# A planner of the instruction order that counts DMA issue time and orders in several passes

## The chip, the cores and the metric

The kernel runs on one core of one Trainium2 chip. The time is the device time of one execution in microseconds (us), median of several runs. TensorE (PE in the profile), VectorE (DVE), ScalarE (ACT), GpSimd (POOL) and SyncE (SP, which issues all the DMAs here) run side by side, each through its own list of instructions in a fixed order. So when an instruction waits, everything behind it on the same engine waits too.

## What is computed

One encoder layer on 1024 + 256 = 1280 tokens of width 1024, in float32: a SwiGLU half step, a token mixing step, a second SwiGLU half step, and a final norm.

```python
h = x + 0.5 * _swiglu(_rmsnorm(x, ffn1_norm), ffn1_w_gate, ffn1_w_up, ffn1_w_down)
...
# mixing: banded attention with a sink (8 heads) beside bidirectional
# retention (4 heads) through one input and one output projection
...
def _swiglu(x, w_gate, w_up, w_down):
    return (jax.nn.silu(x @ w_gate) * (x @ w_up)) @ w_down
```

The hidden width of each SwiGLU is 2816, that is 22 tiles of 128.

## The kernel before

**Arithmetic.** The tokens stand in chunks of 512, 512 and 256 columns (called chunk 0, 1 and 2). Each large product is made of three fast matmuls: both operands are split into a high and a low part (`split`: a cast on ACT makes `xh` or `whi`, a subtraction on DVE makes `xl` or `wlo`), and PE adds xh·whi, xl·whi and xh·wlo. In the two FFNs, seven products stand for eight (`combos` makes sums of activations, `seven` sums of weights), so DVE and ACT have work on every weight tile: `raw` (loaded), `s1` to `s4` (sums, made on DVE), `whi`, `wlo`.

**FFN.** For each of 11 pairs of hidden tiles, gate and up are computed (a wave writes the PSUM banks `pa`; ACT and DVE evict them to `o11`, `o21`, `o22` and `s`), then the activation is split and stored to DRAM in pieces named `a1_<pair>_<piece><h or l>` for FFN1 and `a2_...` for FFN2 (pieces 1, 2, 3, 8, 9, 10 and so on; the profile calls them `a_1l`). Later the down product loads pieces back as `xa` tiles, multiplies them into banks `pb`, and DVE adds those into the residual `h`. The pieces of the last pair are `a1_10_...` and `a2_10_...`; they are stored at the place where gate and up end and the down product starts, called transition 1 (FFN1) and transition 2 (FFN2) below.

**Mixing.** `project` makes the input projection (`lin` products into `pa`), `attention` makes scores, probabilities `prob`, their transposes (PE, into `pb`) and their copies `pt`, `retention` works on blocks, `out_unit` is the output projection.

**Order.** None of this is emitted as it is written. `Weaver` records each operation as an `Op` (`record`, line 172) with a modelled cost (`cost`, line 141) and latency. `order` (line 219) then simulates the five engines: it takes again and again the operation that can start first, and on one engine, among those that could start within `SLACK` of the engine's free time, the one that stands earliest in the program (the heap `now`). It also simulates the slots of the two SBUF pools (77 of 128x512, 66 of 128x256) and of the eight PSUM banks: an operation that needs a new tile waits until a slot is free, and a slot is freed when the last reader of its old tile is done. A DMA reads its `raw` or writes its `a_` piece, so the slot of a stored `xh` or `xl` is free only when its store has landed. SP may run at most `AHEAD` = 300 operations ahead of PE. `emit` (line 364) emits each engine's instructions in the order found. Every instruction of the profile therefore has line 372.

Of the kernel before, what the change touches and what calls it, by code (L numbers as in the profile page):

```python
# [89 lines left out]


class Op:
    __slots__ = ("eng", "calls", "cost", "lat", "bufs", "deps", "idx", "wait", "succ", "ready", "allocs", "kind", "at")

    def __init__(self, eng):
        self.eng, self.calls, self.cost, self.lat, self.bufs, self.deps = eng, [], 0.0, 0.13, {}, set()
# [3 lines left out]
class Weaver:  # L100
# [3 lines left out]

    MARGIN = 0.4
    AHEAD = 300
    ENG = {"tensor": "PE", "vector": "DVE", "scalar": "ACT", "gpsimd": "POOL", "sync": "SP"}

    def __init__(self, tc):
# [30 lines left out]
    @staticmethod  # L140
    def cost(eng, method, a, k, outs, ins):
        n = outs[0].box[3] - outs[0].box[2] if outs else 0
        if eng == "tensor":
            if method == "transpose":
                return 0.107
            r = ins[0].buf.args[2] == F32R
            if r:
                return n / 2400 + 0.0136

            side = outs[0].box[1] - outs[0].box[0] <= 64  # L150
            return max((2.2 if side else 4) * n / 2400, 0.11 if n == 1 else 0.213)
        m = max([n] + [v.box[3] - v.box[2] for v in ins])
        ps = any(v.buf.psum for v in ins)
        if eng == "scalar":
            if a[2:3] == (AF.Identity,):
                return 0.3
            return (0.05 if ps else 0.09) + m * 0.00084 + (0.19 if "accum_out" in k else 0)
        if eng == "gpsimd":
            return 0.3 + n * 0.17
        if method in ("tensor_copy", "tensor_scalar") and not ps:  # L160
            return 0.07 + n * 0.00052 + 0.06 * (len(ins) > 1)
        if method == "tensor_scalar":
            return 0.06 + n * 0.00104 + 0.06 * (len(ins) - 1)
        if method == "tensor_tensor_reduce":
            return 0.13 + n * 0.00104
        if method == "scalar_tensor_tensor":
            return 0.12 + n * 0.00107
        if method == "reciprocal":
            return 0.07 + n * 0.0064
        return 0.07 + m * 0.00104  # L170

    def record(self, calls):
        op = Op(self.ENG[calls[0][0]])
        op.idx = len(self.ops)
        op.calls = calls
        for eng, method, a, k in calls:
            vals = [v for v in list(a) + list(k.values()) if isinstance(v, View)]
            outs = [k["out"]] if "out" in k else [a[0]]
            if k.get("accum_out") is not None:
                outs.append(k["accum_out"])  # L180
            outs = [v for v in outs if isinstance(v, View)]
            ins = [v for v in vals if not any(v is x for x in outs)]
            if method == "dma_start":
                v = (outs + ins)[0]
                nb = (v.box[1] - v.box[0]) * (v.box[3] - v.box[2]) * 4
                op.cost, op.lat, op.kind = 0.05, 2.2, nb
            else:
                op.cost += self.cost(eng, method, a, k, outs, ins)
                f = a[2] if method == "activation" and len(a) > 2 else None
                if f in (AF.Silu, AF.Exp):  # L190
                    op.kind = f
            for views, wr in ((ins, False), (outs, True)):
                for v in views:
                    b = v.buf
                    box = (0, P, 0, b.width) if b.psum else v.box
                    keep = []
                    for x in b.accesses:
                        (p0, p1, c0, c1), i, w = x

                        w = w or b.psum and self.ops[min(i, op.idx - 1)].eng != op.eng  # L200
                        hit = p0 < box[1] and box[0] < p1 and c0 < box[3] and box[2] < c1
                        if hit and (wr or w) and i != op.idx:
                            op.deps.add(i)
                        inside = box[0] <= p0 and p1 <= box[1] and box[2] <= c0 and c1 <= box[3]
                        if not (wr and inside) or i == op.idx:
                            keep.append(x)
                    keep.append((box, op.idx, wr))
                    b.accesses = keep
                    if id(b) not in op.bufs:
                        op.bufs[id(b)] = b  # L210
                        b.left += 1
                        if b.order is None and b.tag is not None:
                            t = self.tags.setdefault(b.tag, {"cap": b.bufs, "bufs": [], "free": [0.0] * b.bufs})
                            b.order = len(t["bufs"])
                            t["bufs"].append(b)
                            op.allocs.append(b)
        self.ops.append(op)

    def order(self):
        import heapq  # L220

        ops = self.ops

        for t in self.tags.values():
            t["seq"], t["live"], t["next"], t["done"] = [0] * len(t["bufs"]), set(), 0, [False] * len(t["bufs"])
# [39 lines left out]
        first = [0]  # L265
# [11 lines left out]
        free = dict.fromkeys(engs, 0.0)  # L277

        later = {e: [] for e in engs}
        now = {e: [] for e in engs}  # L280
# [7 lines left out]
        while len(out) < len(ops):  # L288
            best = None
            for e in engs:  # L290
                lim = free[e] + SLACK
                while later[e] and later[e][0][0] <= lim:
                    heapq.heappush(now[e], heapq.heappop(later[e])[1])
                held = []
                pick = None
                while now[e]:
                    i = heapq.heappop(now[e])
                    if may(ops[i]):
                        pick = (max(free[e], ops[i].ready), i)
                        heapq.heappush(now[e], i)  # L300
                        break
                    held.append(i)
                    if len(held) > 40:
                        break
                for i in held:
                    heapq.heappush(now[e], i)
                if pick is None:
                    for r, i in sorted(later[e])[:40]:
                        if may(ops[i]):
                            pick = (r, i)  # L310
                            break
                if pick is not None:
                    op = ops[pick[1]]
                    start = pick[0]
                    for b in op.allocs:
                        start = max(start, min(self.tags[b.tag]["free"]))
                    if best is None or start < best[0]:
                        best = (start, pick[1], e)
            start, i, e = best
            op = ops[i]  # L320
            if i in now[e]:
                now[e].remove(i)
                heapq.heapify(now[e])
            else:
                later[e].remove((op.ready, i))
                heapq.heapify(later[e])
            for b in op.allocs:
                t = self.tags[b.tag]
                f = min(t["free"])
                t["free"].remove(f)  # L330
                start = max(start, f)
                t["live"].add(b.order)
                t["done"][b.order] = True
                while t["next"] < len(t["done"]) and t["done"][t["next"]]:
                    t["next"] += 1
            cost = op.cost
            if e == "ACT" and op.kind is not None and op.kind != table:
                cost += 1.3
                table = op.kind
            end = start + cost  # L340
            op.at = start
            free[e] = end
            if e == "SP":
                dma = max(dma, end) + op.kind / 390e3
                end = dma
            end += op.lat
            for b in op.bufs.values():
                b.left -= 1
                b.end = max(b.end, end)
                if b.left == 0 and b.tag is not None:  # L350
                    self.tags[b.tag]["free"].append(b.end)
                    self.tags[b.tag]["live"].discard(b.order)
            for s in op.succ:
                x = ops[s]
                x.wait -= 1
                late = 0.0 if x.eng != "PE" else -op.lat if e == "PE" else self.MARGIN
                x.ready = max(x.ready, end + late)
                if x.wait == 0:
                    heapq.heappush(later[x.eng], (x.ready, s))
            out.append(op)  # L360
# [875 lines left out]
```

## Time and profile before

| | |
|---|---|
| runs | 2379.52, 2381.1, 2383.1 us, median 2381.1 |
| profiled execution | 2384.64 us, its span 2382.7 us |
| granted TensorE clock, mean | 0.981 |
| busy | PE 2300.1 us, DVE 1664.0, ACT 1011.8, POOL 28.2 |

The span is the time from the first to the last instruction of the core; the profiled execution's own time is 1.9 us more, and 3.5 us above the median of the runs. Idle time of PE is where a change of order can give or take, as long as PE's work itself stays.

### The profile page before, as it was taken

What the parts mean: (1) busy time and instruction counts of PE and PEld (TensorE: products, weight loads), DVE (VectorE), ACT (ScalarE), POOL (GpSimd) and SP (SyncE); (2) the same over time, 40 slices, a digit from 0 to 9 for tenths busy, and PEclk for the clock granted to TensorE, in tenths of its full rate; (3) what the DMA queues carried; (4) which work ended last, traced back from release to release, by engine and by line L of the source; (5) the groups of instructions that cost most, each with busy time, mean ns of one, the idle gap of its engine ahead of it and who ended that gap; (6) DMA issues with size and microseconds to landing.
All of it is one profiled execution on the core that took longest, in us unless ns stands there. A gap on an engine that the chain in (4) does not pass through costs nothing.

```text
span 2382.7 us, 35970 instructions
## 1 busy us (share of the span) xinstructions
PE 2300.1 (97%) x12354; PEld 1948.1 (82%) x12354; DVE 1664.0 (70%) x3639; ACT 1011.8 (42%) x2297; POOL 28.2 (1%) x31
## 2 busy tenths in 40 slices
PE   7999999999799999999999999999999999989998
PEld 6888888888688888886777878888888888868887
DVE  8677766675777866655677767956776766677866
ACT  6444444443222235235667555534444444322311
POOL 0000000000000000000000000000000000000000
PEclk8999999999899999999999999999999999999999
DMA  4233343338865443230115254223443335876622
GB/s 161 95 123 123 132 147 116 111 114 290 281 197 191 142 154 107 70 106 32 32 43 180 85 168 144 66 100 126 140 153 111 114 122 188 278 250 202 191 81 89
DMA packets 230296, 330.77 MB, mean 139 GB/s; under 512 B 25824, under 2 KB 113760, under 8 KB 230112
## 3 DMA queue, kind: packets, MB, share of 16 engines
q1 hardware_dynamic: 230112, 328.47, 41.2%
q8 instruction: 97, 1.59, 0.3%
q14 instruction: 87, 0.71, 0.1%
HBM read 226.65 MB, written 101.71 MB: 138 GB/s over the span
## 4 chain that ended last, share of the span: by engine, by line
PE 88%; DVE 3%; DMA 3%; ACT 3%; issue 1%; SPq 1%; POOL 0%; POOLq 0%; DVEq 0%; ACTq 0%
PE pa L372 61%; PE pb L372 26%; ACT prob L372 2%; DMA raw<-wf 1%; SPq L372 1%; DVE prob L372 1%; DVE xn L372 1%; DVE wlo L372 1%; ACT whi L372 0%; DVE o L372 0%; DMA xa<-a_7l 0%; PE pc L372 0%; DVE xl L372 0%; ACT pt L372 0%; DVE h L372 0%
## 5 line engine op out<-in xcount | busy, mean ns | idle before, releaser
L372 PE MATMUL pa<-xh,whi 128*128 128x512 f32 (+1 forms) x2576 | 921.6, 358 | 10.3 <-ACT whi L372 3.8
L372 PE MATMUL pa<-xh,wlo 128*128 128x512 f32 (+1 forms) x2576 | 911.8, 354 | 6.1 <-DVE wlo L372 6.0
L372 PE MATMUL pa<-xl,whi 128*128 128x512 f32 (+1 forms) x2576 | 912.1, 354 | 5.6 <-DVE xl L372 5.6
L372 PEld LDWEIGHTS pa<-xh,whi 128*128 128x128 f32 x2576 | 491.5, 191 | 86.7 <-ACT whi L372 8.6
L372 PEld LDWEIGHTS pa<-xh,wlo 128*128 128x128 f32 x2576 | 490.2, 190 | 78.9 <-DVE wlo L372 12.4
L372 PEld LDWEIGHTS pa<-xl,whi 128*128 128x128 f32 x2576 | 491.3, 191 | 69.4 <-DVE xl L372 6.5
L372 PE MATMUL pb<-xa,whi 128*128 128x512 f32 (+1 forms) x1968 | 526.3, 356 | 21.3 <-DVE h L372 18.6
L372 ACT CAST whi<-raw 128x256 fp32r<-128x256 f32 (+1 forms) x676 | 304.3, 473 | 444.1 <-PE pa L372 216.0
L372 PEld LDWEIGHTS pb<-xa,whi 128*128 128x128 f32 x1968 | 349.8, 191 | 77.2 <-DVE h L372 21.9
L372 DVE TENSOR_TENSOR wlo<-raw,whi 128x256 fp32r<-128x256 f32 (+1 forms) x676 | 327.6, 505 | 107.7 <-PE pa L372 53.3
L372 ACT CAST whi<-s 128x256 fp32r<-128x256 f32 x464 | 184.2, 406 | 412.6 <-DVE s L372 211.9
L372 PE MATMUL pb<-xa,wlo 128*128 128x512 f32 (+1 forms) x984 | 348.7, 354 | 3.2 <-DVE wlo L372 3.2
L372 DVE SCALAR_TENSOR_TENSOR h<-pb,h 128x512 f32<-128x512 f32 (+1 forms) x408 | 245.9, 623 | 61.8 <-PE pb L372 59.4
L372 DVE TENSOR_TENSOR wlo<-s,whi 128x256 fp32r<-128x256 f32 x464 | 191.5, 423 | 104.6 <-PE pa L372 53.2
L372 PEld LDWEIGHTS pb<-xa,wlo 128*128 128x128 f32 x984 | 187.5, 191 | 30.9 <-DVE wlo L372 4.4
L372 DVE TENSOR_TENSOR s<-raw,raw 128x256 f32<-128x256 f32 x232 | 97.9, 422 | 86.2 <-PE pa L372 78.7
L372 DVE TENSOR_TENSOR s<-s,raw 128x256 f32<-128x256 f32 x232 | 97.1, 423 | 52.0 <-PE pa L372 34.7
L372 DVE TENSOR_TENSOR o<-o,pa 128x512 f32<-128x512 f32 x120 | 82.2, 685 | 68.9 <-PE pa L372 36.4
L372 ACT ACTIVATE sq<-h 128x512 f32<-128x512 f32 (+1 forms) x96 | 50.4, 555 | 117.1 <-DVE h L372 101.1
L372 ACT CAST xh<-s 128x512 fp32r<-128x512 f32 (+1 forms) x114 | 60.3, 537 | 81.2 <-DVE s L372 56.9
L372 DVE TENSOR_TENSOR xl<-s,xh 128x512 fp32r<-128x512 f32 (+1 forms) x114 | 65.1, 585 | 19.5 <-ACT xh L372 12.7
L372 DVE TENSOR_TENSOR sq<-sq,sq 128x512 f32<-128x512 f32 (+1 forms) x93 | 55.7, 600 | 17.1 <-ACT sq L372 12.8
(126 smaller groups left out, 1644.0 us busy)
## 6 DMA issues: line engine op xcount, KB each, us to landing
raw<-wf SPq DMA_DIRECT2D x464, 128.0 KB, 2.5
raw<-w_in SPq DMA_DIRECT2D x132, 256.0 KB, 3.1
raw<-w_out SPq DMA_DIRECT2D x48, 256.0 KB, 3.1
raw<-wf SPq DMA_DIRECT2D x32, 256.0 KB, 3.6
h<-xT SPq DMA_DIRECT2D x32, 256.0 KB, 5.4
a_1h<-xh SPq DMA_DIRECT2D x22, 256.0 KB, 2.0
a_2h<-xh SPq DMA_DIRECT2D x22, 256.0 KB, 2.1
a_1l<-xl SPq DMA_DIRECT2D x22, 256.0 KB, 2.3
```

Of the source, the lines that this page charges most:

```text
L372: i = getattr(getattr(self.nc, eng), method)(*[r(x) for x in a], **{m: r(x) for m, x in k.items()})
```

## The change

The instructions stay the same ones, 11830 on PE, 3541 on DVE, 2209 on ACT, 27 on POOL and 1598 on SP as the two orders list them; only their order differs. The planner's costs change: an issued DMA keeps SP for 0.47 us where it was 0.05, and lands 2.0 us after its bytes where it was 2.2; a matmul counts as narrow by the smaller of its output's and its operand's partitions; an ACT operation with a tile as scale costs 0.1 more; `bn_stats` costs 0.3. And the order is found in up to four passes. After a pass, `due` walks back from the planned start of each PE operation and gives every other operation the time by which it has to start. The next pass ranks such an operation by the furthest PE operation of the program that was started by then, if that is earlier than its own place. The pass with the shortest modelled span is taken.

```diff
@@ -147,20 +148,23 @@
-            side = outs[0].box[1] - outs[0].box[0] <= 64
+            side = min(outs[0].box[1] - outs[0].box[0], ins[0].box[1] - ins[0].box[0]) <= 64
...
-            return (0.05 if ps else 0.09) + m * 0.00084 + (0.19 if "accum_out" in k else 0)
+            return (0.05 if ps else 0.09) + m * 0.00084 + (0.19 if "accum_out" in k else 0) + (
+                0.1 if isinstance(k.get("scale"), View) else 0)
...
+        if method == "bn_stats":
+            return 0.3
...
-                op.cost, op.lat, op.kind = 0.05, 2.2, nb
+                op.cost, op.lat, op.kind = 0.47, 2.0, nb
...
     def order(self):
+        best, prio = None, list(range(len(self.ops)))
+        for _ in range(self.PASSES):
+            out = self.arrange(prio)
+            if best is None or self.span < best[0]:
+                best = self.span, out
+            due = self.due()
+            at = sorted((op.at, op.idx) for op in self.ops if op.eng == "PE")
+            times, k = [], 0
+            front = 0
+            for t, i in at:
+                front = max(front, i)
+                times.append((t, front))
...
+            prio = []
+            for op in self.ops:
+                if op.eng == "PE" or due[op.idx] is None:
+                    prio.append(op.idx)
+                else:
+                    j = bisect.bisect(times, (due[op.idx], 1 << 60)) - 1
+                    prio.append(min(op.idx, times[max(j, 0)][1]))
+        self.span, out = best
+        return out
+
+    def due(self):
+        due = [None] * len(self.ops)
+        for op in reversed(self.ops):
+            t = None
+            for i in op.succ:
+                s = self.ops[i]
+                x = s.at if s.eng == "PE" else due[i]
+                if x is not None and (t is None or x < t):
+                    t = x
+            if t is not None:
+                due[op.idx] = t - op.cost - op.lat
+        return due
+
+    def arrange(self, prio):
...
-                    heapq.heappush(now[e], heapq.heappop(later[e])[1])
+                    i = heapq.heappop(later[e])[1]
+                    heapq.heappush(now[e], (prio[i], i))
```

Three places show what the new order does. In the rows, the last number of a name is only a counter of the compiled program; the first one names the tile and is the same in both orders.

The first is SP's list at transition 1, where the stores of the last pair stand between the loads of the down product's first pieces. Before:

```order
L372 DMA a1_10_1l_6773<-xl_1605_6760 128x512
L372 DMA xa_1745_6775<-a1_2_5l_2235 128x512
L372 DMA xa_1746_6777<-a1_1_4h_1624 128x512
L372 DMA xa_1747_6779<-a1_1_4l_1653 128x512
L372 DMA xa_1748_6788<-a1_2_4h_2222 128x512
L372 DMA xa_1749_6790<-a1_2_4l_2240 128x512
L372 DMA xa_1754_6792<-a1_1_8h_1436 128x256
L372 DMA xa_1755_6794<-a1_1_8l_1449 128x256
L372 DMA xa_1756_6796<-a1_2_8h_2007 128x256
L372 DMA a1_10_8l_6800<-xl_1613_6786 128x256
L372 DMA xa_1757_6802<-a1_2_8l_2029 128x256
```

With the change, from the first of those stores on:

```order
L433 DMA xa_1754_6716<-a1_1_8h_1425 128x256
L433 DMA xa_1755_6722<-a1_1_8l_1451 128x256
L433 DMA raw_1762_6727<-wf1 128x256
L433 DMA raw_1763_6735<-wf1 128x256
L433 DMA a1_10_1h_6744<-xh_1604_6729 128x512
L433 DMA a1_10_1l_6746<-xl_1605_6739 128x512
L433 DMA a1_10_8h_6755<-xh_1612_6753 128x256
L433 DMA xa_1728_6760<-a1_2_1h_2018 128x512
L433 DMA xa_1729_6770<-a1_2_1l_2034 128x512
L433 DMA a1_10_8l_6779<-xl_1613_6766 128x256
L433 DMA xa_1732_6791<-a1_2_2h_2124 128x512
L433 DMA xa_1733_6799<-a1_2_2l_2139 128x512
```

The store of `xl_1605` moved from SP's row 440 to 428, that of `xl_1613` from 449 to 432; the loads of pieces `a1_2_1` and `a1_2_2` and all that follow now stand behind them. Transition 2 shows the same: the store of `xh_5543` moved from row 1374 to 1344 and that of `xl_5544` from 1383 to 1346.

The second is DVE's list at the start of FFN2, where `wlo_4127` is the low part of the first gate weight, and the `xl_41..` before it are the low parts of the combined activations. Before:

```order
L372 TENSOR_TENSOR xl_4112_16837<-n2_4108_16823,xh_4111_16831 128x512
L372 TENSOR_TENSOR xl_4114_16841<-t3_4109_16829,xh_4113_16835 128x512
L372 TENSOR_TENSOR xl_4116_16843<-t1_4107_16818,xh_4115_16825 128x512
L372 TENSOR_TENSOR xl_4118_16845<-t4_4110_16833,xh_4117_16839 128x512
L372 TENSOR_TENSOR wlo_4127_16847<-raw_4125_16198,whi_4126_16338 128x512
L372 TENSOR_TENSOR wlo_4130_16849<-raw_4128_16305,whi_4129_16383 128x512
```

With the change:

```order
L433 TENSOR_TENSOR xl_3996_16506<-xn_3980_16444,xh_3995_16454 128x512
L433 TENSOR_TENSOR h_1638_6550<-pa_4010_16336,h_1638_6550 128x256
L433 TENSOR_TENSOR h_1639_6602<-pa_4017_16401,h_1639_6602 128x256
L433 TENSOR_TENSOR wlo_4127_16523<-raw_4125_16198,whi_4126_16322 128x512
L433 TENSOR_TENSOR t1_4071_16530<-xn_3910_16145,xn_3973_16364 128x512
L433 SCALAR_TENSOR_TENSOR n2_4072_16535<-t1_4071_16530,xn_3977_16412 128x512
```

`wlo_4127` moved up by 50 rows, in front of the first combination `t1_4071` of the activations, which stood at row 2331 before. PE's list changed with it: bank `pa_4137` (chunk 2) had all its 24 matmuls first; now twelve each of `pa_4137`, `pa_4139` (chunk 0) and `pa_4141` (chunk 1), those which need `whi_4126` and `wlo_4127` alone, stand ahead of the second twelve of `pa_4137`.

The third is ACT's list in a wave of FFN2, around the eviction of bank `pa_4873` by a copy. Before:

```order
L372 CAST xh_4859_20061<-t4_4852_20030 128x512
L372 COPY o11_4882_20069<-pa_4873_19992 128x512
L372 CAST whi_4969_20080<-raw_4930_19682 128x256
L372 CAST whi_4971_20084<-raw_4934_19796 128x256
L372 CAST whi_4973_20108<-raw_4929_19651 128x256
L372 ACTIVATE s_4921_20113<-o11_4882_20069 128x512
L372 ACTIVATE s_4925_20122<-pa_4876_20026 128x256
L372 CAST whi_4975_20124<-raw_4933_19767 128x256
```

With the change:

```order
L433 CAST whi_4969_19993<-raw_4930_19767 128x256
L433 CAST whi_4971_19995<-raw_4934_19920 128x256
L433 CAST whi_4973_20002<-raw_4929_19755 128x256
L433 CAST whi_4975_20016<-raw_4933_19812 128x256
L433 CAST xh_4853_20024<-n2_4850_20009 128x512
L433 CAST xh_4855_20029<-t3_4851_20014 128x512
L433 CAST xh_4857_20041<-t1_4849_20004 128x512
L433 CAST xh_4859_20051<-t4_4852_20022 128x512
L433 COPY o11_4882_20062<-pa_4873_19986 128x512
L433 CAST whi_5018_20068<-raw_5005_19961 128x256
```

The four weight casts `whi_4969` to `whi_4975` stood behind the copy, and stand ahead of it now.

## Rows read from the trace of the kernel before

**Rows 1.** The page, busy time of each engine.

```profile
PE 2300.1 (97%) x12354; PEld 1948.1 (82%) x12354; DVE 1664.0 (70%) x3639; ACT 1011.8 (42%) x2297; POOL 28.2 (1%) x31
```

**Rows 2.** Waits of PE: us in total, times, longest us.

```profile
PE pb L372 <- DVE h L372: 18.6, 6, 8.2
PE pb L372 <- ACT prob L372: 10.5, 9, 2.5
...
PE pa L372 <- DVE xl L372: 5.6, 2, 3.8
...
PE pb L372 <- ACT pt L372: 4.7, 8, 0.7
```

**Rows 3.** Windows: stretch, length, busy PE PEld DVE ACT POOL, PEclk, DMA share, GB/s.

```profile
597.60:640.80 43.20, 29.17 (x126) 23.16 (x124) 29.35 (x60) 9.84 (x27) 0.00 (x0) 0.76 0.98 342
640.80:684.00 43.20, 43.20 (x225) 36.98 (x226) 36.35 (x82) 7.70 (x20) 0.00 (x0) 1.00 0.38 120
1100.00:1300.00 200.00, 185.63 (x1206) 139.92 (x1204) 135.83 (x422) 131.39 (x337) 7.33 (x7) 0.96 0.20 65
...
1560.00:2060.00 500.00, 500.00 (x2640) 431.49 (x2639) 328.38 (x693) 218.49 (x502) 0.00 (x0) 1.00 0.42 139
...
2080.00:2110.00 30.00, 20.16 (x91) 16.10 (x90) 17.28 (x35) 6.54 (x20) 0.00 (x0) 0.83 0.99 346
```

**Rows 4.** Timeline of SP's queue before transition 2: start, us, instruction.

```profile
2054.17 0.32 SPq L372 DMA_DIRECT2D xa<-a_3h  x1
...
2064.01 0.38 SPq L372 DMA_DIRECT2D xa<-a_8h  x1
2064.49 0.38 SPq L372 DMA_DIRECT2D a_1h<-xh  x1
```

**Rows 5.** Timeline, FFN1 wave: start, us, instruction [idle before <-releaser].

```profile
232.69 0.40 ACT L372 CAST whi<-raw 128x256 fp32r<-128x256 f32 x1 [2.20 <-DMA raw<-wf]
...
233.09 0.43 DVE L372 TENSOR_TENSOR wlo<-raw,whi 128x256 fp32r<-128x256 f32 x1 [1.56 <-DMA a_8h<-xh]
...
234.37 0.50 PE L372 MATMUL pa<-xh,whi 128*128 128x512 f32 x1 [1.57 <-DVE o L372]
```

**Rows 6.** Timeline, all engines, transition 1.

```profile
587.06 0.32 SPq L372 DMA_DIRECT2D xa<-a_6h  x1
...
589.06 0.42 DVE L372 TENSOR_TENSOR xl<-s,xh 128x256 fp32r<-128x256 f32 x1
...
600.41 0.62 ACT L372 CAST xh<-s 128x512 fp32r<-128x512 f32 x1 [7.24 <-DMA a_1l<-xl]
...
601.03 0.32 SPq L372 DMA_DIRECT2D a_8l<-xl  x1
...
605.18 0.76 DVE L372 TENSOR_TENSOR wlo<-s,whi 128x256 fp32r<-128x256 f32 x2 [3.09 <-DMA a_8l<-xl]
```

**Rows 7.** Timeline of PE in the mixing step, first head.

```profile
1113.37 0.95 PE L372 MATMUL pb<-ident,prob 128*128 128x128 f32 x4 [2.52 <-ACT prob L372]
```

**Rows 8.** Timeline of PE, start of FFN2.

```profile
1544.75 0.58 PE L372 MATMUL pa<-xh,wlo 128*128 128x256 f32 x1 [5.66 <-DVE wlo L372]
```

**Rows 9.** Timeline, all engines, transition 2.

```profile
2071.14 0.93 ACT L372 CAST xh<-s 128x512 fp32r<-128x512 f32 x2 [1.20 <-DVE s L372]
...
2089.56 0.38 SPq L372 DMA_DIRECT2D a_9h<-xh  x1
...
2092.68 0.43 DVE L372 TENSOR_TENSOR s<-s,raw 128x256 f32<-128x256 f32 x1 [8.76 <-DMA a_9h<-xh]
...
2093.76 1.22 PE L372 MATMUL pb<-xa,whi 128*128 128x512 f32 x2 [8.24 <-DVE h L372]
```

**Rows 10.** Timeline, FFN2 wave, eviction of `pa_4873` and what follows.

```profile
1827.76 0.58 ACT L372 COPY o<-pa 128x512 f32<-128x512 f32 x1
...
1831.08 0.40 PE L372 MATMUL pa<-xh,whi 128*128 128x512 f32 x1
...
1831.67 0.40 ACT L372 CAST whi<-raw 128x256 fp32r<-128x256 f32 x1
```

More of the change, by code (lines that the diff above doesn't have):

```diff
@@ L92 @@
 class Op:
-    __slots__ = ("eng", "calls", "cost", "lat", "bufs", "deps", "idx", "wait", "succ", "ready", "allocs", "kind", "at")
+    __slots__ = ("eng", "calls", "cost", "lat", "bufs", "deps", "idx", "wait", "succ", "ready", "allocs", "kind", "at", "first")
     def __init__(self, eng):
@@ L106 @@
     AHEAD = 300
+    PASSES = 4
     ENG = {"tensor": "PE", "vector": "DVE", "scalar": "ACT", "gpsimd": "POOL", "sync": "SP"}
@@ L216, in record @@
                             op.allocs.append(b)
+        op.first = list(op.allocs)
         self.ops.append(op)
     def order(self):
+        best, prio = None, list(range(len(self.ops)))
[10 more added lines that the diff above has]
+                times.append((t, front))
+            import bisect
+            prio = []
[20 more added lines that the diff above has]
+    def arrange(self, prio):
         import heapq
         ops = self.ops
+        for op in ops:
+            op.succ, op.ready, op.at = [], 0.0, None
+            op.allocs = list(op.first)
+            for b in op.bufs.values():
+                b.left = 0
+                b.end = 0.0
+        for op in ops:
+            for b in op.bufs.values():
+                b.left += 1
+        for t in self.tags.values():
+            t["free"] = [0.0] * t["cap"]
         for t in self.tags.values():
@@ L296, in order @@
                 while now[e]:
-                    i = heapq.heappop(now[e])
+                    x = heapq.heappop(now[e])
+                    i = x[1]
                     if may(ops[i]):
                         pick = (max(free[e], ops[i].ready), i)
-                        heapq.heappush(now[e], i)
+                        heapq.heappush(now[e], x)
                         break
-                    held.append(i)
+                    held.append(x)
                     if len(held) > 40:
@@ L320, in order @@
             op = ops[i]
-            if i in now[e]:
-                now[e].remove(i)
+            if (prio[i], i) in now[e]:
+                now[e].remove((prio[i], i))
                 heapq.heapify(now[e])
```

## The prediction

> **What bounds the kernel now.** I read the busy times first, then PE's waits, then PE stretch by stretch, and last the stretches in which PE idles with every engine beside it. PE is busy 2300.1 us of a span of 2382.7 [rows 1], so the whole idle time of PE is 82.6 us. Work on PE is the same before and after, so an order can win at most this, plus what the clock loses after idle time. DVE is next with 1664.0 us (70%) and matters only in places.
>
> Where the 82.6 us are: PE waits longest for DVE's additions into the residual `h`, 18.6 us in 6 waits, then for `prob` (10.5), for `xl` (5.6, of which 3.8 in one wait) and `pt` (4.7) [rows 2]. By stretches, the gate and up waves of FFN2 have no idle time at all: 500.00 busy of 500.00 us. The idle time stands at the two transitions, in the mixing step (185.63 of 200 us busy, so 14.4 idle) and in single waits [rows 3]. For the transitions I take the pace of the undisturbed stretch that follows the first: 225 matmuls in 43.2 us, 0.192 us each. Transition 1 has 126 matmuls in 43.2 us, worth 24.2 us, so it loses 19.0. Transition 2 has 91 in 30 us, worth 17.5, so it loses 12.5 [rows 3]. Both hold a lower clock too (0.76 and 0.83 against 1.00), which this counting includes.
>
> Why the transitions stall is seen across engines. At transition 1 the low part of piece 8, `xl`, is made by 589.48 and its store issued at 601.03, because SP sends loads in the program's order meanwhile. The slot stays taken: DVE waits for that store until 605.18. ACT waited 7.24 us, until 600.41, for the store of piece 1 [rows 6], with the weight casts for the down product behind it. At transition 2 the cast of piece 9 ends by 2072.07, its store goes out at 2089.56, DVE waits 8.76 us for the slot, and PE 8.24 us for the addition into `h` that stands behind on DVE [rows 9].
>
> **The change, part by part.** No instruction is added or removed. Everything below is a move, priced by the stall it meets. The planner itself costs no device time.
>
> *DMA issue counted as 0.47 us.* SP's issues that wait for nothing are 0.48 us apart (2064.01 to 2064.49) [rows 4], so the new number describes the chip and the old 0.05 did not: the old plan believed that SP had sent a long run of loads at once, and so put no price on a store standing behind them. The Trainium skill, DMA: Bandwidth & Descriptors, section "Anatomy of one DMA — SWDGE (gpsimd) path", splits the fixed cost and gives the sequencer's dispatch about 50 ns. By that figure the old 0.05 would be right, and the new plan would space the loads too far apart; the transitions would gain nothing (21 us of the sum below) and the time be about 2367. The trace's 0.48 us decides against it, and the section is about GpSimd's path, not SP's; I give it no chance of its own.
>
> *Transition 1.* The stores of pieces 1 and 8 move from SP's rows 440 and 449 to 428 and 432, ahead of the loads of the second pair. So the slots come free before ACT and DVE reach the tiles that need them. The stall can't vanish: DVE has 29.35 us of work in the stretch against 24.2 of PE's [rows 3]. With DVE as the bound the stretch takes 29.35 and not 43.2 us, 13.85 less. I take **−13** (bounds: 0, if another slot is late; −19.0, if DVE's work finds room earlier).
>
> *Transition 2.* The same move by 30 rows of SP for the `xh` of piece 9. DVE has 17.28 us of work for PE's 17.5 [rows 3], so it could keep up, but only without any wait. I take two thirds of the loss, **−8** (bounds 0 and −12.5). The loads moved behind the stores are covered by a queue that runs far ahead; if that cover is gone, see the second rival.
>
> *Start of FFN2.* PE waits 5.66 us for `wlo_4127` [rows 8], which stood last on DVE, behind all combinations. It stands 50 rows earlier now, and PE takes 36 matmuls that need this unit alone first: 12 of 256 columns and 24 of 512. At the mean of FFN2's waves (500 us for 2640 matmuls, 0.19 us) [rows 3] they are 6.8 us of work, in which DVE can reach the other units' parts, still at the end of its list. I take **−6**, the wait and a little of the clock that drops after it (bounds 0 and −7.5).
>
> *FFN1 waves.* In one wave ACT stood 2.20 us waiting for a load, for a cast that stood ahead of an eviction; DVE stood 1.56 us for a store, with its own part of that eviction behind; PE then waited 1.57 us [rows 5]. The new order has the eviction ahead on both engines. The same swap stands in two more waves; with half the gain each it is **−3** (bounds 0 and −5).
>
> *Start.* The largest wait for `xl`, 3.8 us [rows 2], falls in the first chunk's product: DVE did five normalisations before the first two `xl`. These now stand ahead of them, at the price of later ones. **−2** (0 to −3.8).
>
> *Mixing step.* PE idles 14.4 us there [rows 3]. Its order changes: for the first head a projection (`pa_2954`, 18 matmuls) goes between the transposes of `prob`, where the 2.52 us wait stood [rows 7]; for the second head `pa_3009` goes ahead of them; for the third head nothing comes between. A product put into a gap is missing somewhere later, so I take **−6** (bounds +5, if the moved products leave a later gap bare that is as large as two of these waits, and −14.4).
>
> *FFN2 waves.* PE has no idle time there to win, only something to lose. In 68 of the 96 evictions between the start of FFN2 and transition 2, ACT now has weight casts ahead that stood behind, 140 casts in all (in 19 evictions it lost 28). In the example the copy of a bank starts at 1827.76 and ends at 1828.34, and PE writes that bank again at 1831.08: 2.74 us of slack. Four casts of 0.31 to 0.41 us ahead of it take 1.2 to 1.6 us and fit, if their slots are free [rows 10]. I allow **+3** for waves in which they don't (bounds 0 and +58, the third rival).
>
> Sum: −13 − 8 − 6 − 3 − 2 − 6 + 3 = **−35 us**. The profiled execution took 2384.64 us (span 2382.7 and 1.9 around it), so its like would take 2349.6; it lies 3.5 us above the median of the runs, so against the median of 2381.1 I predict **2346 us**.
>
> **The rivals.**
>
> *DVE bounds the transitions.* Only half of their 21 us comes back, because the additions into `h` queue behind the splits that now start earlier. For it: DVE has 29.35 us of work against PE's 24.2, and 17.28 against 17.5 [rows 3]. Against it: the long idle times of DVE and ACT there are waits for slots, not for its own work [rows 6, 9]. Time: 2346 + 10.5, about 2356.
>
> *Stores block SP.* SP takes its list in order, so a store placed before its tile is made holds all loads behind it. At transition 2 the first store of the last pair now stands where SP was at 2054.17 before; that store went out at 2064.49 [rows 4], so SP may stand still up to 10 us, with the DMA engines at 0.99 in what follows [rows 3]. At transition 1 SP would reach the store at about 587.06 and the tile of piece 8 is made at 589.48 [rows 6], so about 2 us. If the lost 12 us of issuing all reach PE through late loads, the time is 2346 + 12, about 2358, and with DVE's rival together about 2368. Against it: SP sends these loads well ahead of PE's first use of them, which covers a part. The Trainium skill, same page and section, says that a DMA's wait on a semaphore happens on the issuing sequencer before dispatch, which is this mechanism; the trace agrees so far that SP's queue stands behind waits, but no row shows a store holding a needed load.
>
> *Casts ahead of evictions make the FFN2 waves stall: slower.* Place: ACT in the about 18 waves between 1560 and 2060. If the moved casts can't start before their slot is free, as the last of the four in the example, which ran from 1831.67 to 1832.07 before, the copy behind it ends at about 1832.7, 1.6 us after PE wants its bank at 1831.08 [rows 10]. Two such evictions in each of 18 waves are 58 us: 2346 + 58, about 2404. It decides from 2.2 us per wave (40 us in all) on. For it: so many casts moved ahead. Against it: the loads of the next unit moved behind the stores on SP, so slots for the casts come free earlier, and the planner simulates slots and banks.
>
> *The change does nothing.* If the first pass, ranked as before, won and only the costs counted, orders might differ off the path alone: 2381. Against it: the moves stand exactly where PE idles.
>
> **How the numbers follow.** Chances: the forecast 0.50, DVE bound 0.19, SP blocked (alone or with it) 0.13, slower 0.13, nothing 0.05. With every gain at its far bound and no loss in the waves the sum is −62.2 (19 + 12.5 + 7.5 + 5 + 3.8 + 14.4), or 2319; all at once is unlikely, so the range begins at 2324. It ends at **2374**, above both rivals together (2368), and leaves out no change and slower, 18 in 100. Two runs of this kernel differ by up to 0.15%, so 0.2% (4.8 us) is about what can be told from no change. Faster by more than that: 0.82. Within: 0.05. Slower: 0.13.
>
> **What would show it.** Right: the stretch from the end of gate and up in FFN1 loses no more than 6 us against 0.192 us per matmul, no wait of ACT or DVE on a store over 2 us at either transition, the 5.66 us wait at the start of FFN2 gone, PE's wait for `h` in total under 8 us, FFN2's waves still at full busy time. Wrong: PE waiting for `o` or `s` evictions in the waves (third rival); SP standing in front of a store while PE waits for `xa` or a cast waits for `raw` (second); DVE without idle time while PE waits for `h` (first). A gap in the mixing step as large as those filled would make that one term wrong.

## The result and the profile after

The changed kernel takes 2339.99 us (median of 4 runs, 2339.66 to 2342.69), the kernel before 2381.02 us; the ratio is 0.983, interval 0.9813 to 0.9847. The forecast was 2346 us in a range of 2324 to 2374. The profiled execution took 2342.69 us, its span 2340.8 at a mean clock of 0.987, so the two profiled spans differ by 41.9 us.

The page of the changed kernel, busy times, answers to [rows 1]:

```profile
PE 2285.1 (98%) x12354; PEld 1947.0 (83%) x12354; DVE 1665.2 (71%) x3639; ACT 1014.0 (43%) x2297; POOL 28.1 (1%) x31
```

PE's idle time fell from 82.6 to 55.7 us. That is 26.9 of the 41.9; the rest is in PE's busy time, which fell by 15.0 us with the same matmuls. A part of that is the clock (0.987 on average, 0.981 before), a part is weights that came late before, shown below. PE's waits after (total, times, longest) answer to [rows 2]:

```profile
PE pb L433 <- ACT prob L433: 7.6, 3, 3.3
PE pb L433 <- ACT pt L433: 6.9, 12, 0.9
...
PE pb L433 <- DVE h L433: 5.0, 4, 2.4
...
PE pb L433 <- ACT y L433: 2.6, 1, 2.6
PE pb L433 <- DVE mx L433: 2.5, 2, 2.1
PE pa L433 <- DVE xl L433: 2.4, 2, 1.9
```

The wait for the additions into `h` fell from 18.6 to 5.0 us and the wait of 5.66 us for `wlo` at the start of FFN2 is gone. The mixing step's waits (`prob`, `pt`, `y`, `mx`) did not fall in sum: 7.6 + 6.9 + 2.6 + 2.5 us, against 10.5 + 4.7 for `prob` and `pt` and 0.2 for `y` before. Windows of the changed kernel: the first and the third hold the work of transition 1 and transition 2 in [rows 3]; the second holds FFN2's waves and goes on to where the third begins:

```profile
583.57:609.88 26.31, 23.88 (x125) 19.63 (x123) 25.70 (x53) 6.17 (x16) 0.00 (x0) 1.00 1.00 352
...
1528.60:2048.80 520.20, 517.80 (x2729) 447.08 (x2728) 348.96 (x746) 229.43 (x526) 0.00 (x0) 1.00 0.43 147
2048.83:2065.61 16.78, 16.78 (x90) 14.44 (x89) 16.40 (x32) 2.14 (x6) 0.00 (x0) 1.00 0.96 338
```

The 43.2 us of transition 1 became 26.31 and the 30 us of transition 2 became 16.78, both at full clock (1.00). The 2.40 us of idle time in the second window are a wait for `h` at its end, which belongs to transition 2; the waves themselves are still busy throughout. SP's queue at transition 1 shows why it became shorter:

```profile
577.02 0.33 SPq L433 DMA_DIRECT2D a_1l<-xl  x1
...
579.40 0.38 SPq L433 DMA_DIRECT2D a_8l<-xl  x1
```

PE enters the stretch at 583.57, so these stores now go out 4 to 7 us before it; before, PE entered the same work at 597.6 and the store of piece 8 left at 601.03 [rows 6]. In the changed kernel no wait of ACT or DVE at either transition is put down to a store. The casts wait for something else instead: for weights that are still to be loaded (`raw`), 20.0 us in transition 1 and 20.3 in transition 2, against nothing and 0.3 before. PE felt little of that: it waits 3.6 and 4.2 us there, against 13.9 and 10.6 before.

**Where the time came from, by stage.** The program's stages are cut by sets of PE instructions (all that had started before 60, 594.6, 673.5, 1070, 1500, 1566, 2061 and 2142 us in the kernel before), and each stage ends when the last of its set starts (the rest with PE's last instruction). The differences to the kernel before, in us, profiled executions; the columns from the third on are the experiments below, in their order (issue cost alone, passes alone, both, all costs in one pass, the three small costs, the stores by hand, the landing time, and three issue costs).

| stage | before | changed | dma | passes | dma+passes | costs | narrow | scale | bn | stores | landing | 0.25 | 0.65 | 0.94 |
|---|---|---|---|---|---|---|---|---|---|---|---|---|---|---|
| start | 59.8 | −2.5 | +0.9 | −2.3 | −2.8 | −1.3 | −2.8 | −1.6 | −3.3 | +0.3 | −3.0 | −2.4 | −2.6 | +3.8 |
| FFN1 waves | 534.8 | −11.6 | −8.3 | −5.7 | −11.5 | −8.2 | −11.5 | −11.6 | −11.5 | −0.7 | −10.1 | −2.0 | −11.2 | −11.5 |
| transition 1 | 78.8 | −14.6 | −12.5 | +6.7 | −13.0 | −12.7 | −13.8 | −15.7 | −13.8 | −12.2 | −13.4 | −8.2 | −17.3 | −2.4 |
| FFN1 down | 396.5 | −0.5 | −2.7 | +0.8 | −2.3 | −2.7 | −2.3 | −0.5 | −2.4 | +0.6 | −2.6 | +0.5 | −2.3 | −5.5 |
| mixing | 430.1 | +2.8 | −1.5 | −1.5 | −3.2 | +5.0 | −0.5 | +3.4 | +2.3 | −1.3 | −2.2 | +1.6 | −3.6 | −2.5 |
| start of FFN2 | 65.8 | −7.7 | +0.7 | −7.7 | −7.7 | +0.6 | −7.7 | −7.7 | −7.7 | +0.2 | −7.7 | −7.7 | −6.6 | −6.6 |
| FFN2 waves | 494.7 | −0.2 | −0.2 | 0.0 | −0.2 | −0.2 | −0.2 | −0.2 | −0.2 | 0.0 | −0.2 | +4.0 | −0.2 | −0.2 |
| transition 2 | 81.3 | −6.4 | −7.1 | +14.8 | −8.1 | −8.6 | −8.0 | −7.4 | −7.6 | −3.2 | −6.4 | −2.6 | −10.8 | +4.2 |
| rest | 233.7 | −1.2 | −3.2 | +0.7 | −1.2 | −2.4 | −0.9 | −1.4 | −1.4 | −1.4 | −1.7 | −0.4 | −2.4 | −5.6 |

### The profile page after: what moved, and what is told of

Read it like the earlier page. It is cut to its first block, busy times and chain, and to the rows that moved or that the text cites. A ratio compares the mean times of both kernels' runs of the same rounds, so it can differ in the third digit from the quotient of the medians.

```text
span 2340.8 us, 35831 instructions
## 1 busy us (share of the span) xinstructions
PE 2285.1 (98%) x12354; PEld 1947.0 (83%) x12354; DVE 1665.2 (71%) x3639; ACT 1014.0 (43%) x2297; POOL 28.1 (1%) x31
## 4 chain that ended last, share of the span: by engine, by line
PE 92%; DVE 3%; ACT 2%; DMA 2%; issue 1%; SPq 0%; POOL 0%; POOLq 0%; DVEq 0%; ACTq 0%
PE pa L433 63%; PE pb L433 28%; PE pc L433 1%; DMA h<-xT 1%; ACT prob L433 1%; DMA raw<-wf 1%; DVE wlo L433 1%; DVE xn L433 1%; DVE s L433 0%; ACT pt L433 0%; DVE h L433 0%; DVE xl L433 0%; SPq L433 0%; DVE prob L433 0%; DMA xa<-a_3h 0%
## 5 line engine op out<-in xcount | busy, mean ns | idle before, releaser
L433 ACT ACTIVATE o<-pa 128x512 f32<-128x512 f32 (+1 forms) x92 | 53.8, 584 | 32.3 <-PE pa L433 32.1
```

What stands on the lines that cost most here:

```text
L433: i = getattr(getattr(self.nc, eng), method)(*[r(x) for x in a], **{m: r(x) for m, x in k.items()})
```

## The experiments

Times are medians; ratios with intervals are against the kernel before on the same chip (three chips, on which it took 2382.3 to 2382.9).

**The parts of the change.** Theory A: the issue cost of 0.47 us puts the stores ahead at the transitions and the evictions ahead in FFN1's waves; the passes repair the start of FFN2. Rival B: the due times carry the gain. Rival C: one of the three small costs does something of its own.

*Issue cost and landing time alone.*

```diff
-                op.cost, op.lat, op.kind = 0.05, 2.2, nb
+                op.cost, op.lat, op.kind = 0.47, 2.0, nb
```

> The planner of before with one line changed: a DMA issue costs 0.47 us and lands 2.0 us after its bytes (one pass, no due times). Theory A (the issue cost moves the stores at both transitions and the evictions in FFN1's waves; the passes move the start of FFN2 and the start of the kernel): transitions -14.5 and -6, FFN1's waves -10, nothing at the start of FFN2, so about 2351 us, with the 5.7 us wait at the start of FFN2 still there. Rival B (the due times of the later passes carry the gain): 2372 to 2381 us.

2350.53 us (2344.91 to 2350.94), ratio 0.9861 (0.9848 to 0.9875): theory A to within 1 us in total. The stages it named gave 12.5, 7.1 and 8.3 us, where it had 14.5, 6 and 10; the stages it did not name gave another 6. The wait at the start of FFN2 is still there, as in [rows 8] (PE's waits of this run):

```profile
PE pa L372 <- DVE wlo L372: 6.2, 3, 5.7
```

*Passes alone.* The changed kernel with its five cost edits taken back:

```diff
-                op.cost, op.lat, op.kind = 0.47, 2.0, nb
+                op.cost, op.lat, op.kind = 0.05, 2.2, nb
...
-            side = min(outs[0].box[1] - outs[0].box[0], ins[0].box[1] - ins[0].box[0]) <= 64
+            side = outs[0].box[1] - outs[0].box[0] <= 64
```

and the terms for `scale` and `bn_stats` removed.

> The four passes with due times, all costs as before (issue 0.05 us). Theory A: start of FFN2 -8 and start of the kernel -3, transitions unchanged, so about 2370 us, with ACT still waiting over 5 us for a store at transition 1. Rival B: about 2345 us.

2390.53 us, ratio 1.0036 (1.0023 to 1.0048): slower, which neither theory expected. The start of FFN2 gave its 7.7 us as in theory A, and FFN1's waves gave 5.7, so what the two parts are worth there overlaps; but transition 2 lost 14.8 and transition 1 6.7. PE and DVE of this run at transition 2:

```profile
2090.86 1.22 PE L430 MATMUL pb<-xa,whi 128*128 128x512 f32 x2 [21.91 <-DVE h L430]
```

```profile
2089.78 0.43 DVE L430 TENSOR_TENSOR wlo<-s,whi 128x256 fp32r<-128x256 f32 x1 [25.59 <-DMA a_9h<-xh]
```

DVE waited 25.59 us for the store of piece 9, where it was 8.76 us before [rows 9]: the new order of DVE came to that slot at about 2064 already, with the additions that PE needs behind it. Why the plan took that order for a good one is not shown. It is not blind to late stores: the planner counts the bytes of all loads sent earlier into the time at which a store lands, at any issue cost (more on this below).

*Issue cost and passes, without the three small costs.*

```diff
-            side = min(outs[0].box[1] - outs[0].box[0], ins[0].box[1] - ins[0].box[0]) <= 64
+            side = outs[0].box[1] - outs[0].box[0] <= 64
```

and the terms for `scale` and `bn_stats` removed.

> The issue cost of 0.47 us and the four passes, the other three costs (narrow matmuls, scale from a tile, bn_stats) as before. Theory A: all of the gain, 2340 us within 4. Rival C (the other costs set the order in the mixing step and are worth something there): off by over 5 us, in the mixing step alone.

2334.57 us, ratio 0.98 (0.9787 to 0.9814): all of the gain, and 5.4 us more than the change itself, which is more than theory A allowed (4 us) and is what rival C said. The stages say where: the mixing step (−3.2 here, +2.8 in the change), while no other stage differs by more than 1.8.

*All costs, one pass.*

```diff
-    PASSES = 4
+    PASSES = 1
```

> All new costs, one pass. Theory A: as the issue cost alone, about 2351 us, within 4. Rival B: 2372 to 2381. Rival C: over 5 us from the run with the issue cost alone, in the mixing step.

2354.21 us, ratio 0.9882 (0.9868 to 0.9895). Against the issue cost alone it is 3.7 us slower, again in the mixing step (+5.0 against −1.5). With all the new costs the passes are worth 14.2 us (2354.21 to 2339.99), with the issue cost alone 16.0 (2350.53 to 2334.57); with the old costs they lose 8.

**The small costs one by one,** each added to the run of 2334.57 us. C1, C2 and C3 stand in the expectations.

```diff
+            side = min(outs[0].box[1] - outs[0].box[0], ins[0].box[1] - ins[0].box[0]) <= 64
```

> The issue cost and the passes (2334.6 us), plus the changed cost of narrow matmuls alone. Theory C1 (this cost reorders PE in the mixing step and makes the 5.4 us between 2334.6 and 2340): 2339 to 2341, the difference standing in the mixing step. Theory C2 (any of the small costs gives the same, since each only shuffles near ties): all three of these runs within 2 us of 2337. Theory C3 (the scale cost does it, the only one that also moves the FFNs): 2334.6 within 2.

```diff
+                0.1 if isinstance(k.get("scale"), View) else 0)
```

> The issue cost and the passes (2334.6 us), plus 0.1 us for an ACT operation with a tile as scale. C1: 2334.6 within 2. C2: about 2337. C3: 2339 to 2341, with a part of it outside the mixing step.

```diff
+        if method == "bn_stats":
+            return 0.3
```

> The issue cost and the passes (2334.6 us), plus 0.3 us for bn_stats. It moves rows from the mixing step on and none of SP's. C1 and C3: 2334.6 within 2. C2: about 2337.

2337.33 us (0.9809, 0.9794 to 0.9825), 2340.74 (0.982, 0.9803 to 0.9836) and 2338.72 (0.9813, 0.9797 to 0.983). All three are slower than 2334.57 by 2.8 to 6.2 us and in the mixing step by 2.7 to 6.6; C1 and C3 fall, C2 is nearest, with a spread wider than it said. No run of the three is as fast as the slowest of the 2334.57 us kernel (2335.86), but the intervals of the ratios overlap with its interval and with each other, so neither the order among the three nor the size of each loss is settled.

**The late stores by hand.** The kernel, planner and costs of before; only SP's list is changed after planning, by moving the `xa` loads that stand up to so many places ahead of each store of the last pair behind that store.

```diff
-        return out
+        return self.stores_first(out)
+    UP = {"1l": 16, "8l": 24, "3h": 18, "3l": 18, "2h": 24, "2l": 26, "9h": 24, "9l": 29, "10h": 28, "10l": 29}
...
+                for x in sp[max(0, j - up):j]:
+                    if any(b.args[4].startswith("xa") for b in x.allocs):
+                        late[x.idx] = max(late.get(x.idx, 0), j)
```

> The kernel of before with its planner and costs as they were; only on SP, the loads of the down product that stand ahead of the last pair's stores are put behind them (16 to 29 places, both transitions). ACT, DVE and PE keep their order. Theory A (the late stores are the cause of the stalls at the transitions): transition 1 -12, transition 2 -7, everything else 0, so about 2363 us. Rival (the order of ACT and DVE that came with it is what helps): above 2373. Rival (loads that stand behind the stores come late): PE waits for xa, and the time is above 2363 by as much.

2367.99 us, ratio 0.9935 (0.9921 to 0.9949). Transition 1 gave 12.2 us with ACT, DVE and PE in their old order, as theory A said, and no other stage moved by more than 1.5. Transition 2 gave only 3.2. The edit moves no weight loads, and there the stores still stood behind eight of them (SP, then ACT, of this run):

```profile
2063.18 5.77 SPq L405 DMA_DIRECT2D raw<-wf  x8
2069.06 0.38 SPq L405 DMA_DIRECT2D a_2h<-xh  x1
2070.00 0.44 SPq L405 DMA_DIRECT2D a_9h<-xh  x1
```

```profile
2074.36 0.41 ACT L405 CAST whi<-s 128x256 fp32r<-128x256 f32 x1 [12.37 <-DMA a_9h<-xh]
```

ACT waited 12.37 us for the same store, and PE 6.58 us for a `whi` that ACT made after it, so the same cause was half left in place.

**How much issue cost.** Four variants of the run of 2334.57 us, in one line: landing 2.2, and issue 0.25, 0.65 and 0.94.

```diff
-                op.cost, op.lat, op.kind = 0.47, 2.0, nb
+                op.cost, op.lat, op.kind = 0.47, 2.2, nb
```

> The issue cost of 0.47 us and the passes as in the run of 2334.6 us, but a DMA lands 2.2 us after its bytes, as before. Theory A (the issue cost, not the landing time, carries the gain at the transitions): transitions as at 2334.6, all together 2332 to 2342, any difference being shuffles in the mixing step. Rival D (the landing time matters): transitions lose over 5 us.

2338.62 us (0.9817, 0.9804 to 0.9831): transition 1 within 0.4 us, transition 2 with 1.7 us less gain. The landing time doesn't carry the gain.

```diff
+                op.cost, op.lat, op.kind = 0.25, 2.0, nb
```

> As the run of 2334.6 us, but an issue counts 0.25 us. The stores of the last pair stand at SP's rows 435 and 436 (transition 1) and 1370 (transition 2), against 428, 431 and 1344 at 0.47, and 440, 449 and 1374 before. Theory A: most of transition 2's stall is back (6 to 15 us) and some of transition 1's (3 to 10), so 2345 to 2360. Rival (only the ranking matters): 2334.6 within 4.

2366.26 us (0.9925, 0.9912 to 0.9939), 6 us outside the expectation: transition 1 lost 4.8 us of its gain, as said, and transition 2 5.5, a little less than said; but FFN1's waves lost 9.5, the mixing step 4.8, FFN2's waves 4.2 and FFN1's down product 2.8.

```diff
+                op.cost, op.lat, op.kind = 0.65, 2.0, nb
```

> As the run of 2334.6 us, but an issue counts 0.65 us, the spacing while the DMA engines are full. The stores stand at SP's rows 410, 411 and 1335. Theory A (once slots come free in time, earlier stores bring nothing more): transitions within 3 us of those at 2334.6, total 2332 to 2342. Rival E (stores ahead of their tiles hold SP, and loads come late): transitions lose over 5 us, PE or ACT waits for loads, total above 2342.

2327.13 us (0.9769, 0.9755 to 0.9782), better than expected and the best kernel of the study: transition 1 gave 17.3 us and transition 2 10.8, together 7.0 more than in the run of 2334.57 us (issue 0.47). That the transitions had nothing more to give was wrong. But stores were not what was left: neither kernel has a wait of ACT or DVE for a store over 0.8 us there. What shrank is the casts' wait for weights. ACT at transition 1, at 0.47 and then at 0.65 us (waits in total, times, longest):

```profile
ACT whi L430 <- DMA raw<-wf: 22.1, 9, 12.9
```

```profile
ACT whi L430 <- DMA raw<-wf: 2.9, 3, 1.4
```

At transition 2 it fell from 18.6 to 10.4 us, and PE's waits at the two transitions fell from 2.9 and 4.3 us to 0.7 and 1.0.

```diff
+                op.cost, op.lat, op.kind = 0.94, 2.0, nb
```

> As the run of 2334.6 us, but an issue counts 0.94 us, twice what the trace shows. The stores stand at SP's rows 403, 405 and 1320. Theory A: the planner now spaces loads that could go closer together, but the engines run as fast as the chip lets them, so at most 10 us are lost, 2335 to 2347. Rival E: SP stands in front of stores at both transitions, 2350 to 2370.

2358.94 us (0.99, 0.9887 to 0.9914): rival E. This run is not like its neighbours in one respect: the planner's first pass has the shortest modelled span here (2358.6, then 2360.6, 2363.3 and 2363.2 us), so its order is one without due times, while in the other runs with four passes a later pass was taken. Its like at 0.47 us is therefore the run of 2350.53 us. SP's queue from 550 to 600 us of this run, waits in total, times, longest:

```profile
SPq L430 <- ACT xh L430: 11.7, 4, 4.6
...
SPq L430 <- DVE s L430: 3.9, 2, 2.8
...
SPq L430 <- DVE xl L430: 1.7, 4, 0.7
```

and what followed, on all engines:

```profile
592.76 0.44 SPq L430 DMA_DIRECT2D a_9l<-xl  x1
593.25 3.79 SPq L430 DMA_DIRECT2D raw<-wf  x8
595.63 0.94 ACT L430 CAST whi<-raw 128x256 fp32r<-128x256 f32 x2 [3.99 <-DMA raw<-wf]
```

SP stood 11.7 us in front of stores whose `xh` was not made. The weight loads left behind the last of them, ACT waited 3.99 us for the first, and PE in turn waited 5.8 us for `whi`. At transition 2 it was the same: SP waited 13.9 us for `xh` and PE 7.0 us for `whi`. In the changed kernel SP's queue lists no wait for `xh` in the same stretch.

## Why the prediction came out as it did

The forecast of 2346 us held (2340), by a sum whose terms were partly wrong in opposite ways: FFN1's waves gave 8.6 us more than forecast and the mixing step 8.8 less, and it is luck that these cancel. The signs that were to show the mechanism came: transition 1 loses 2.3 us against 0.192 us per matmul, no wait on a store is left at the transitions, the wait at the start of FFN2 is gone, PE's wait for `h` is 5.0 us and FFN2's waves are busy throughout. One sign of the second rival came too, casts that wait for `raw`, though without SP standing in front of a store.

- **Transition 1, −13:** measured −14.6, and −12.2 with nothing but SP's list changed. Shown. The bound by DVE was a little too strict: DVE still fills the stretch (25.70 of 26.31 us), but with 3.7 us less work in it than the 29.35 that I left there: seven of its 60 instructions ran before the stretch.
- **Transition 2, −8:** measured −6.4. The stretch itself lost all of its stall (16.78 us, busy throughout), 13.2 us less than before. About half of that came back around it. Ahead of it PE waits 2.40 us for `h`, and the clock granted from 2039 to 2046 us is 0.76 on average; the work there takes 2.9 us more than before. Behind it the same matmuls take 3.4 us more, with waits for late weights. In one of them a cast waits for its load, and PE for the cast:

```profile
2094.53 0.40 ACT L433 CAST whi<-raw 128x256 fp32r<-128x256 f32 x1 [5.16 <-DMA raw<-wf]
...
2095.30 0.74 PE L433 MATMUL pb<-xa,whi 128*128 128x512 f32 x2 [0.81 <-ACT whi L433]
```

- **Start of FFN2, −6:** measured −7.7, and −7.7 from the passes alone with the old costs. One pass at 0.47 us gave nothing there. The first-pass order at 0.94 us gave 6.6, so the due times are not the only way to it.
- **Start, −2:** −2.5.
- **FFN1 waves, −3:** measured −11.6. This is the step of the prediction that failed: the term was mis-sized most, and with it fell the first statement, that an order can win at most PE's idle time and what the clock loses after it. From 60 to 580 us, before and after, PE's clock was at 1.00 and its idle time only 4.0 us before:

```profile
60.00:580.00 520.00, 515.99 (x2680) 437.11 (x2679) 350.83 (x761) 236.53 (x526) 0.00 (x0) 1.00 0.39 132
```

```profile
60.00:580.00 520.00, 519.93 (x2735) 448.09 (x2735) 361.99 (x784) 238.97 (x536) 0.00 (x0) 1.00 0.41 139
```

  In the same 520 us PE did 55 more matmuls. I had counted the idle gaps of three waves, two of them at half. The rest was hidden in PE's busy time: weight loads (PEld) that waited for their weights. PE's weight loads between 60 and 580 us, before:

```profile
PEld pa L372 <- DVE wlo L372: 5.5, 17, 0.5
PEld pa L372 <- ACT whi L372: 4.7, 16, 0.9
PEld pa L372 <- DVE o L372: 4.6, 6, 1.8
```

and after:

```profile
PEld pa L433 <- DVE wlo L433: 0.4, 1, 0.4
PEld pa L433 <- DVE o L433: 0.3, 1, 0.3
PEld pa L433 <- ACT whi L433: 0.3, 1, 0.3
```

  14.8 us of such waits became 1.0. The waits for banks (`o`) are the gaps that I priced; those for `wlo` and `whi`, 33 waits of 0.3 us, show as next to no idle time of PE, since a matmul is still running or counted as running. They cost less than their 10.2 us. In this stage PE's matmuls of 512 columns mostly start 0.227 us apart and those of 256 columns 0.120; what goes beyond that sums to 13.3 us before and 1.7 after. Of the 13.3, 6.5 stand at PE's idle gaps and in the eleven matmuls behind each, and 5.6 at late weight loads without such a gap, counted in the same way. That these moved with the order is shown; which move on DVE, ACT or SP made the weights come earlier is not.
- **Mixing step, −6:** measured +2.8, a loss where the forecast had a gain, within the bound of +5 that I named. What the rows show is that bound's mechanism: the filled gap moved. PE of the changed kernel:

```profile
1188.76 1.20 PE L433 MATMUL pb<-ident,prob 128*128 128x128 f32 x4 [3.27 <-ACT prob L433]
...
1262.98 0.33 PE L433 MATMUL pb<-ident,y 128*128 128x128 f32 x1 [2.56 <-ACT y L433]
```

  The wait of 2.52 us in [rows 7] is gone, and a wait of 3.27 us stands at a later head. Over the change and its twelve variants this stage lies between −3.6 and +5.0 us, and each of the small costs alone moves it by 2.7 to 6.6. What decides among near ties there stays open.
- **FFN2 waves, +3:** measured −0.2. The rival that the moved casts stall the evictions did not happen. ACT and PE around the example of [rows 10]:

```profile
1788.68 1.02 ACT L433 CAST whi<-raw 128x256 fp32r<-128x256 f32 x3 [0.75 <-PE pa L433]
...
1793.26 0.58 ACT L433 COPY o<-pa 128x512 f32<-128x512 f32 x1
...
1797.04 0.40 PE L433 MATMUL pa<-xh,whi 128*128 128x512 f32 x1
```

  The casts ran from 4.6 us ahead of the copy on, in time that ACT had free, and the copy ended 3.2 us before PE wants the bank (2.74 before). Only at an issue cost of 0.25 us did these waves lose anything (4.0 us).
- **The rivals.** *DVE bounds the transitions* was right as a limit and wrong as a loss. *Stores block SP* did not happen at 0.47 us and did at 0.94: the mechanism is real and was only not reached. The Trainium skill, DMA: Bandwidth & Descriptors, section "Anatomy of one DMA — SWDGE (gpsimd) path", says that a DMA's semaphore wait happens on the issuing sequencer, and that run's 11.7 us on SP agree. The 50 ns of dispatch that this section of the Trainium skill gives, taken as the planner's issue cost, is the run with passes and old costs: it took 2390.53 us, where the prediction worked out about 2367.
- **What the issue cost does.** I wrote that the old plan put no price on a store standing behind a long run of loads. That was wrong. The planner sends all bytes through one queue of 390 GB/s at any issue cost (`dma = max(dma, end) + op.kind / 390e3`). In the times that it models, the store of `xl_1613` lands 14.5 us after it is issued in the old plan, 4.6 in the new one and 3.0 with 0.65 us. The old 14.5 is near what happened: the data was made at 589.48 and DVE went on at 605.18 [rows 6]. But the planner sends each load as soon as SP is free and a slot is there, and never holds one back for a store that is still to come. So a larger issue cost also works as a brake, which leaves fewer loads in front of a store. Whether the better orders come from a truer price or from this brake was not separated by any run.

## What to carry to other kernels

A list scheduler is only as good as its cost table: the same ranking by due times gained 14 to 16 us with the issue time counted at what the trace shows, and lost 8 with issues counted as nearly free. Where one queue carries both loads and the stores that free slots, read when a store's data was made and when it was issued; a late store stalls whoever needs the slot, a store placed too early stalls the queue, and here the best of the five costs tried was 0.65 us. And look at the waits of the weight loads as well as PE's: of the 13.3 us that PE lost in FFN1's waves, 5.6 stood in no idle gap.

## What the hardware showed that was not expected

The cost that served best is not the 0.48 us of a free queue [rows 4] but 0.65, near the spacing of issues in the stretches that matter: with the DMA engines full (a share of 1.02 from 2070 to 2080 us), SP's issues before were 0.65 us apart (kernel before, transition 2):

```profile
2070.76 0.32 SPq L372 DMA_DIRECT2D xa<-a_7h  x1
2071.41 0.32 SPq L372 DMA_DIRECT2D xa<-a_7l  x1
```

That this match is the reason for the gain is argued, not shown: a larger cost also holds loads back, and a run with the cost made to depend on the queue's load was not made.
